# Two entries of a fused encoder layer reordered: norm, T2 and B11 ahead of weight sums and B22; token loads ahead of residual rows and later weight rows

## The chip, the core and the metric

The kernel runs on one NeuronCore of a Trainium2 chip. TensorE (PE) multiplies, VectorE (DVE), ScalarE (ACT) and GpSimd (POOL) do the elementwise work, and all loads and stores are issued in order by SyncE (SP), whose queue feeds 16 DMA engines. The metric is device time in microseconds (us) of one execution, the median over runs.

## The reference

One layer of a streaming encoder runs over 1024 prompt tokens and 8 x 16 sample tokens, 1152 token columns in all, model width 1024, in fp32. The change touches the second half of the layer:

```
x = x + g1 * mix                                   # residual after the output projection
h = rms_norm(x, norm_ffn) * (1 + sc2) + sh2        # per-token norm, modulation
up, ffn_new = causal_dwconv(h @ w_up, ffn_prev, conv_ffn_w, conv_ffn_b)
u, gt = jnp.split(up, 2, axis=-1)                  # 2816 columns each
x = x + g2 * ((jax.nn.silu(gt) * u) @ w_down)
```

## The kernel before, in words

Tokens lie along the free axis, features along the partitions. Every fp32 product is made of three passes over rounded operands: a value is split into a high part (cast on ACT) and a low part (value minus high part, on DVE), and PE adds high x high, low x high and high x low. A 128 x 576 product over 512 features is thus 24 matmuls (`product`).

Up projection. The 1024 x 1152 activations are cut into four quarters X11, X21 (first 576 tokens, features 0-511 and 512-1023) and X12, X22 (last 576 tokens). One Winograd-like step of seven products (P1 to P7) replaces eight. It needs the operands B11, B21, B22 (splits of X11, X21, X22) and T1 to T4 (splits of sums of quarters: T3 from X12 - after X22 - X12 -, T2 from X11 + that, T4 from X21 - T2, T1 from X22 - T2). `tsums` makes the sums, `halves` splits a quarter.

The first 768 tokens are complete before the last third (`out_proj(2, ...)`) is projected; their scaling, modulation and the splits of B11 and B21 are done piece by piece in `both`, which `hook` advances after each of that projection's eight outputs. The last third needs its own norm first (a column sum on PE, a power on POOL, a replication on PE, then `mod2` on DVE and ACT). Until T1 to T4 exist, PE is fed with the part of the work that needs B11 and B21 alone: `fill(0)` to `fill(5)`, each the P1 and P2 products of one early weight pair (48 matmuls). Then `Pair` objects run in the order `seq`; `prep` makes weight sums (`sums`) and splits (`wop`) up to LA = 3 steps ahead of `run`. The first products in `seq` are of pair 6: P1 (B11), P6 (T2), P5 (T1), P7 (T3), P2 (B21), P4 (T4).

P1, P6, P7 and P4 of a pair add to one PSUM bank, and each intermediate value is copied out by ACT (`evac` into a buffer of `tm4`) before the next product may add to it. The tile `tm4` takes one of the four quarter buffers when its quarter and T4's low part are no longer used; T1l, T3l and T4l take the other three.

Down projection. It is cut in the same way, over 11 pairs of feature blocks: `SEQ` runs P1, P6, P7, P4, P2, P5, P3, each for m = 0 to 10, 24 matmuls for each m. `dload` loads the gated activations `gd` (into the five `raw` buffers, two for each m of P6) and, for P1, P6 and P7, the rows of w_down: WA in P1 (names wa), WB[m][1] (wbh) and WB[m][0] (wbl). `dprep` makes sums and splits. After P1, P6 and P7 the four accumulators are copied to `pbuf`; `fma` later adds them to residual rows, which `resid` loads from DRAM (1152 KB each, xr). A residual load was traced at m = 6 and the `fma` steps at m = 1 to 4 of the next product.

The order on each engine isn't that of the code. A scheduler places the traced instructions by priorities and readiness; `tc.issue_after(ins)` obliges it to place what the block traces on the engine of `ins` behind `ins`. Each engine then runs its list strictly in its order.

Of the kernel before, what the change touches and what calls it, by code (L numbers as in the profile page):

```python
# [10 lines left out]
ALU = mybir.AluOpType  # L11
# [9 lines left out]
HT = 576  # L21
# [3 lines left out]
KD = 11  # L25
# [14 lines left out]
def body(ctx, tc, d):  # L40
    nc = tc.nc
    V, S, G_, T = nc.vector, nc.scalar, nc.gpsimd, nc.tensor
# [258 lines left out]
    def traced():  # L301
        return nc.cur_bb.bb.instructions[-1]
# [532 lines left out]
    h = [R(), R()]  # L835
# [80 lines left out]
    def quarter(nm, dt=F32):  # L916
        return ha.tile([P, 4, HT], dt, name=nm, tag="X", bufs=4)

    X11, X21, X12, X22 = (quarter("X" + n) for n in ("11", "21", "12", "22"))
    M2 = mod[:, 24:32, :]  # L920

    def split(op, x, ks):
        S.copy(op[0][:, ks, :], x[:, ks, :])  # L923
        V.tensor_tensor(op[1][:, ks, :], x[:, ks, :], op[0][:, ks, :].bitcast(F32), op=ALU.subtract)

    def tsums(c):
        V.tensor_tensor(X12[:, :, c], X22[:, :, c], X12[:, :, c], op=ALU.subtract)
        V.tensor_tensor(X11[:, :, c], X11[:, :, c], X12[:, :, c], op=ALU.add)
        V.tensor_tensor(X21[:, :, c], X21[:, :, c], X11[:, :, c], op=ALU.subtract)

    def both():
        for g in range(2):
            for kt in range(8) if g == 0 else scaled(1):
                xs = x1k[g][kt // 4][:, kt % 4, :]
                x1, x2 = ((X11, X12), (X21, X22))[kt // 4]
                parts = [(x1[:, kt % 4, 0:GN], xs)] if g == 0 else [
                    (x1[:, kt % 4, GN:HT], xs[:, 0:192]), (x2[:, kt % 4, 0:192], xs[:, 192:GN])]
                for o, x in parts:
                    S.activation(o, x, AF.Identity, bias=M2[:, kt, 0:1])
# [28 lines left out]
    fso = wt([P, 44, 18], "fso")  # L968

    nops = [0]  # L970
    cur, evs = [], {}

    def wop(x):
        i = nops[0] % 2
# [30 lines left out]
    def fill(j):  # L1005
        u = rawt()
        nc.sync.dma_start(out=u[:, :1024], in_=d["w_up"][2 * j])
        X = bank("P1")
        product(X, wop(u[:, 0:512]), B11)
        pc = wt([P, NT], "uy", 2)  # L1010
        p, c = pc[:, 0:HT], pc[:, HT:NT]
        S.copy(two(p), bk(X))
        nc.sync.dma_start(out=p1d[j], in_=p)
        Y = bank("P2")
        product(Y, wop(u[:, 512:1024]), B21)
        V.tensor_tensor(two(c), two(p), bk(Y), op=ALU.add)
        nc.sync.dma_start(out=c11d[j], in_=c)
# [17 lines left out]
    def halves(nm, x, l):  # L1035
        h = hi[nm]
        for k0 in (0, 2):
            split((h, l), x, slice(k0, k0 + 2))
        return h, l

    fill(0)
    fill(1)
    rb = bank("rst")
    for t in range(3):
        T.matmul(rb[:, 0, t:t + 1], ss2[:, t * P:(t + 1) * P], C["ones"][:, 0:1], start=True, stop=True)
    r2 = rstd2[:, 2, :]
# [9 lines left out]
    tsums(slice(192, HT))  # L1056
    fill(4)
    T2 = halves("T2", X11, hi["T2l"])
    B22 = halves("B22", X22, hi["B22l"])
    V.tensor_tensor(X22, X22, X11, op=ALU.subtract)  # L1060
    fill(5)
    T1 = halves("T1", X22, quarter("T1l", F32R))
    T3 = halves("T3", X12, quarter("T3l", F32R))
    T4 = halves("T4", X21, quarter("T4l", F32R))
    tm4 = quarter("tm4")
# [146 lines left out]
    for i in range(len(seq)):  # L1212
        while loaded < len(firsts) and firsts[max(loaded - 1, 0)] <= i + 1:
            seq[firsts[loaded]][0].load()
            loaded += 1
        while prepped < min(len(seq), i + 1 + LA):
            seq[prepped][0].prep(seq[prepped][1])
            prepped += 1
        seq[i][0].run(seq[i][1])
    hs_.close()  # L1220
# [19 lines left out]
    def wload(k, t, c):  # L1240
        nc.sync.dma_start(out=t, in_=d["w_down"][k, :, c])

    def dload(s):
        n, m = SEQ[s]
        if n == "P1":
            wload(K1[m], WA[m][:, lo_], lo_)
        raws[s] = []
        for kk, c in SRC[n]:
            r = rawt()
            nc.sync.dma_start(out=r[:, :HT], in_=gd[kk[m], :, c])  # L1250
            raws[s].append(r)
        if n == "P1":
            wload(K1[m], WA[m][:, hi_], hi_)
        elif n == "P6":
            wload(K2[m], WB[m][1], hi_)
        elif n == "P7":
            wload(K2[m], WB[m][0], lo_)

    def bop(x):
        h = dl.tile([P, HT], F32R, name="gh", tag="gh", bufs=4)  # L1260
# [44 lines left out]
    def advance(upto):  # L1305
        ev = None
        while st["prepped"] < min(len(SEQ), upto):
            while st["loaded"] < min(len(SEQ), st["prepped"] + 4):
                n, m = SEQ[st["loaded"]]
                if held() + len(SRC[n]) > 5:  # L1310
                    break
                dload(st["loaded"])
                st["loaded"] += 1
            ev = dprep(st["prepped"])
            st["prepped"] += 1
        return ev

    def resid(t, r, c):
        nc.sync.dma_start(out=t, in_=x1d[:, 4 * r:4 * r + 4, c])
        return t  # L1320
# [55 lines left out]
    for s in range(nt):  # L1376
        n, m = SEQ[s]
        advance(s + 1 + LA)
        if m == 0 and n in ("P1", "P2", "P5"):
            acc = [bank("acc") for _ in range(4)]  # L1380
        if m == 6 and n in ("P1", "P6", "P7"):
            xr[HOME[n]] = resid(xrs.pop(0), *HOME[n])
        if m == 6 and n == "P4":
            xr[FIN[n]] = resid(pbuf, *FIN[n])
        if 0 < m <= 4 and hold:
            h, p = hold[0]
            fma(xr[h][:, m - 1, :], m - 1, *h, p=p[:, m - 1, :])
            if m == 4:
                hold.clear()
        if s < nt - TAIL:  # L1390
            for o in range(4):
                dmul(acc, s, o)
        elif s == nt - 1:
            for o in range(4):
                for q in range(nt - TAIL, nt):
                    dmul(acc, q, o)
        if m < KD - 1:
            continue
        if n in HOME:
# [117 lines left out]
```

## Time and profile before

| | |
|---|---|
| median of 3 runs | 1293.63 us (1288.19 to 1293.78) |
| the profiled execution's own time | 1292.55 us |
| its span, first to last instruction | 1290.3 us |
| mean granted TensorE clock | 0.979 |
| PE busy / DVE / ACT / POOL | 96% / 75% / 49% / 15% of the span |
| DMA | 218.71 MB, 49.4% of 16 engines' span in the hardware queue |

All times of the trace are counted from the span's start. 525 us is where the first `fill` product starts, 1030.6 us where the down projection starts. 2.25 us of the execution lie outside the span.

### The profile page before, as it was taken

How to read it: one execution, taken by the hardware profiler on the slowest of the kernel's cores; microseconds unless marked ns; L12 is line 12 of the kernel's file. 1: busy time of each engine (PE TensorE's matmuls, PEld its weight loads, DVE VectorE, ACT ScalarE, POOL GpSimd, SP SyncE). 2: the span in 40 equal slices, each digit the busy share in tenths (PEclk: the TensorE clock that was granted, in tenths of full speed). 3: DMA queues.
4: the chain of work that ended last, by engine and by line, in shares of the span. 5: the costliest groups of instructions: out<-in, count | busy, mean ns of one | idle time of the engine just before them, and what ended most of it. 6: DMA issues, size and time to landing. Idle time of an engine off the chain costs nothing.

```text
span 1290.3 us, 22870 instructions
## 1 busy us (share of the span) xinstructions
PE 1238.4 (96%) x8813; PEld 1161.9 (90%) x8813; DVE 962.3 (75%) x1920; ACT 627.7 (49%) x1111; POOL 193.8 (15%) x242
## 2 busy tenths in 40 slices
PE   5899989999999999989999999999999998999998
PEld 3698769888887999988999999999999997999998
DVE  3497798565885675796999888876867578986664
ACT  3367736665566534564444444545444444443332
POOL 0031554343420330000111101000000000000000
PEclk8999989999999989989999999999999998999999
DMA  8785443887586488621333232221212498434341
GB/s 321 285 289 197 153 147 123 289 288 265 196 301 251 151 288 315 201 97 59 106 106 103 96 109 91 83 92 62 94 53 73 150 357 293 123 110 152 122 129 60
DMA packets 87708, 218.71 MB, mean 170 GB/s; under 512 B 14928, under 2 KB 27344, under 8 KB 87600
## 3 DMA queue, kind: packets, MB, share of 16 engines
q1 hardware_dynamic: 87600, 217.26, 49.4%
q8 instruction: 69, 1.13, 0.4%
q14 instruction: 39, 0.32, 0.1%
HBM read 175.81 MB, written 41.42 MB: 168 GB/s over the span
## 4 chain that ended last, share of the span: by engine, by line
PE 80%; DVE 9%; DMA 6%; ACT 2%; issue 2%; POOL 0%; SPq 0%; DVEq 0%; ACTq 0%
PE P L990 36%; PE acc L1354 16%; PE s_f L305 3%; PE s_f L307 3%; PE s_f L306 3%; PE out_proj L305 2%; PE out_proj L306 2%; PE out_proj L307 2%; PE attn_o L547 1%; PE ada L154 1%; DMA wbh<-in_w_down 1%; DMA xs<-in_xT 1%; PE attn_t L534 1%; DVE PT L667 1%; PE s_q L305 1%
## 5 line engine op out<-in xcount | busy, mean ns | idle before, releaser
L990 PE MATMUL P<-T,wh 128*128 128x288 f32 x704 | 206.7, 296 | 7.4 <-ACT T L923 3.9
L990 PE MATMUL P<-T,wl 128*128 128x288 f32 x704 | 207.9, 296 | 0.0
L1354 PE MATMUL acc<-gh,wl 128*128 128x288 f32 x616 | 182.5, 299 | 0.7 <-DVE wl L981 0.7
L1354 PE MATMUL acc<-gh,wh 128*128 128x288 f32 x616 | 176.6, 298 | 5.2 <-ACT wh L979 5.2
L1354 PE MATMUL acc<-gl,wh 128*128 128x288 f32 x616 | 179.6, 297 | 0.0
L990 PEld LDWEIGHTS P<-T,wh 128*128 128x128 f32 x704 | 132.5, 189 | 8.3 <-ACT tm L1133 4.2
L990 PEld LDWEIGHTS P<-T,wl 128*128 128x128 f32 x704 | 133.2, 189 | 0.0
L1097 DVE SCALAR_TENSOR_TENSOR uy<-uraw,fw,uy 128x1024 f32<-128x1024 f32 x88 | 112.2, 1278 | 22.9 <-ACT uy L1094 22.9
L981 DVE TENSOR_TENSOR wl<-raw,wh 128x512 fp32r<-128x512 f32 x143 | 94.9, 685 | 38.2 <-ACT wh L979 38.2
L1354 PEld LDWEIGHTS acc<-gh,wh 128*128 128x128 f32 x616 | 115.0, 190 | 5.6 <-ACT wh L979 5.6
L1354 PEld LDWEIGHTS acc<-gh,wl 128*128 128x128 f32 x616 | 117.5, 191 | 0.9 <-DVE wl L981 0.9
L1354 PEld LDWEIGHTS acc<-gl,wh 128*128 128x128 f32 x616 | 117.0, 191 | 0.0
L81 ACT CAST wh<-raw 128x1024 fp32r<-128x1024 f32 (+1 forms) x72 | 75.8, 1053 | 57.8 <-PE out_proj L307 30.7
L979 ACT CAST wh<-raw 128x512 fp32r<-128x512 f32 x143 | 83.4, 620 | 38.6 <-PE P L990 34.2
L1262 ACT CAST gh<-raw 128x576 fp32r<-128x576 f32 x66 | 44.4, 675 | 111.8 <-PE acc L1354 94.0
L1263 DVE TENSOR_TENSOR gl<-raw,gh 128x576 fp32r<-128x576 f32 x66 | 49.7, 756 | 50.0 <-ACT gh L1262 49.7
L1133 ACT COPY tm<-P 128x576 f32<-128x576 f32 x47 | 29.8, 635 | 113.7 <-PE P L990 102.6
L305 PE MATMUL s_f<-Rh,wh 128*128 128x384 f32 x240 | 83.2, 347 | 0.0
L307 PE MATMUL s_f<-Rl,wh 128*128 128x384 f32 x240 | 82.2, 342 | 0.0
L306 PE MATMUL s_f<-Rh,wl 128*128 128x384 f32 x240 | 81.8, 341 | 0.0
L1099 POOL COPY fso<-uraw 128x2 f32<-128x2 f32 x44 | 13.3, 303 | 447.7 <-DVE uraw L1082 447.7
L305 PE MATMUL out_proj<-Rh,wh 128*128 128x384 f32 x192 | 67.8, 354 | 0.9 <-ACT qn L424 0.9
(382 smaller groups left out, 3549.1 us busy)
## 6 DMA issues: line engine op xcount, KB each, us to landing
raw<-in_w_up SPq DMA_DIRECT2D x50, 512.0 KB, 3.4
raw<-gd SPq DMA_DIRECT2D x88, 288.0 KB, 2.8
raw<-in_w_ada SPq DMA_DIRECT2D x32, 512.0 KB, 5.8
raw<-in_w_f SPq DMA_DIRECT2D x30, 512.0 KB, 6.2
gd<-uy SPq DMA_DIRECT2D x22, 576.0 KB, 3.2
raw<-in_w_out SPq DMA_DIRECT2D x24, 512.0 KB, 5.1
wl<-low_f SPq DMA_DIRECT2D x20, 512.0 KB, 4.5
raw<-in_w_ad SPq DMA_DIRECT2D x16, 512.0 KB, 5.6
```

The costliest lines, as they stand in the source:

```text
L81: S.copy(wh[:, :n], raw[:, :n])
L305: T.matmul(ps, lh, rh, start=first, stop=False)
L306: T.matmul(ps, ll, rh, start=False, stop=False)
L307: T.matmul(ps, lh, rl, start=False, stop=last)
L979: S.copy(h, x)
L981: V.tensor_tensor(l, x, h.bitcast(F32), op=ALU.subtract)
L990: T.matmul(ps[:, c, 0:HC], x[:, m], y[:, kt, cc], start=first and kt + n == 0, stop=kt == 3 and n == 2, skip_group_check=True)
L1097: V.scalar_tensor_tensor(y[:, :1024], raw[:, j:j + 1024], k[:, j:j + 1], y[:, :1024], op0=ALU.mult, op1=ALU.add)
L1133: S.copy(two(dst), bk(ps))
L1262: S.copy(h, x)
L1263: V.tensor_tensor(l, x, h.bitcast(F32), op=ALU.subtract)
L1354: T.matmul(acc[o][:, c, 0:HC], x[:, oc], y[:, cc], start=first and i == 0, stop=m == KD - 1 and i == 2, skip_group_check=True)
```

## The change

At the first entry `both` goes through one feature block of both token groups at a time; the last term of `tsums` (X21, for T4) becomes `tsum4`; the norm's column sum is traced between `fill(0)` and `fill(1)`; X21, B22 and X22 are placed behind T2, weight steps 0 to 2 behind T2, and all later ones behind T1. At the second entry the rows wbh are loaded four m earlier in P1 (m > 3) and the remaining ones in P6, the residual rows are loaded at P6 m = 1, P7 m = 1, P7 m = 8 and P4 m = 7 instead of P1, P6, P7 and P4 m = 6, and the `fma` steps move from m = 1..4 to m = 7..10 (m = 3..6 in P4). The arithmetic is the same.

```diff
     def tsums(c):
         V.tensor_tensor(X12[:, :, c], X22[:, :, c], X12[:, :, c], op=ALU.subtract)
         V.tensor_tensor(X11[:, :, c], X11[:, :, c], X12[:, :, c], op=ALU.add)
+
+    def tsum4(c):
         V.tensor_tensor(X21[:, :, c], X21[:, :, c], X11[:, :, c], op=ALU.subtract)
 
     def both():
-        for g in range(2):
-            for kt in range(8) if g == 0 else scaled(1):
+        s1 = scaled(1)
+        for kt in range(8):
+            for g in range(2):
+                if g == 1:
+                    next(s1)
...
     fill(0)
-    fill(1)
     rb = bank("rst")
     for t in range(3):
         T.matmul(rb[:, 0, t:t + 1], ss2[:, t * P:(t + 1) * P], C["ones"][:, 0:1], start=True, stop=True)
     r2 = rstd2[:, 2, :]
     V.tensor_scalar(r2, rb[:, 0, 0:3], 1.0 / 1024, EPS, op0=ALU.mult, op1=ALU.add)
     G_.tensor_tensor(r2, r2, C["expo"][:, :3], op=ALU.pow)
+    fill(1)
...
     T2 = halves("T2", X11, hi["T2l"])
-    B22 = halves("B22", X22, hi["B22l"])
-    V.tensor_tensor(X22, X22, X11, op=ALU.subtract)
+    ev2 = traced()
+    with tc.issue_after(ev2), tc.issue_after(evs["ACT"]):
+        tsum4(slice(192, HT))
+        B22 = halves("B22", X22, hi["B22l"])
+        V.tensor_tensor(X22, X22, X11, op=ALU.subtract)
     fill(5)
     T1 = halves("T1", X22, quarter("T1l", F32R))
+    ev1 = traced()
...
         while prepped < min(len(seq), i + 1 + LA):
-            seq[prepped][0].prep(seq[prepped][1])
+            with tc.issue_after(ev2 if prepped < 3 else ev1):
+                seq[prepped][0].prep(seq[prepped][1])
...
+        evs["SP"] = traced()
         if n == "P1":
             wload(K1[m], WA[m][:, hi_], hi_)
-        elif n == "P6":
-            wload(K2[m], WB[m][1], hi_)
-        elif n == "P7":
-            wload(K2[m], WB[m][0], lo_)
+        with tc.issue_after(evs["SP"]):
+            if n == "P1" and m > 3:
+                wload(K2[m - 4], WB[m - 4][1], hi_)
+            elif n == "P6" and m < 4:
+                wload(K2[m + 7], WB[m + 7][1], hi_)
+            elif n == "P7":
+                wload(K2[m], WB[m][0], lo_)
...
-        if m == 6 and n in ("P1", "P6", "P7"):
-            xr[HOME[n]] = resid(xrs.pop(0), *HOME[n])
-        if m == 6 and n == "P4":
-            xr[FIN[n]] = resid(pbuf, *FIN[n])
-        if 0 < m <= 4 and hold:
+        for h in {("P6", 1): [HOME["P1"]], ("P7", 1): [HOME["P6"]], ("P7", 8): [HOME["P7"]]}.get((n, m), []):
+            with tc.issue_after(evs["SP"]):
+                xr[h] = resid(xrs.pop(0), *h)
+        m0 = 3 if n == "P4" else KD - 4
+        if m0 <= m < m0 + 4 and hold:
             h, p = hold[0]
-            fma(xr[h][:, m - 1, :], m - 1, *h, p=p[:, m - 1, :])
-            if m == 4:
+            with tc.issue_after(evs["DVE"]):
+                fma(xr[h][:, m - m0, :], m - m0, *h, p=p[:, m - m0, :])
+            if m == m0 + 3:
                 hold.clear()
```

Where the rows stand on the engines. VectorE around the last third's norm, before (uy is a `fill` result, rstd2 the norm's sum, wl a low part of weights, S1 a weight sum, L1023 the first step of `mod2`):

```order
L1016 TENSOR_TENSOR uy_5624<-uy_5624,P2_5627 128x576
L981 TENSOR_TENSOR wl_5817<-raw_5813,wh_5816 128x512 x2
L1016 TENSOR_TENSOR uy_5687<-uy_5687,P2_5690 128x576
L1047 TENSOR_SCALAR rstd2_91<-rst_5719 128x3
L981 TENSOR_TENSOR wl_5883<-raw_5879,wh_5882 128x512 x2
L1125 TENSOR_TENSOR S1_6136<-raw_6035 128x512
L1023 SCALAR_TENSOR_TENSOR X12_5197<-X12_5197,A2_80,rst_5719 128x256 x4
```

The same place after the change (L1032 is the first step of `mod2`):

```order
L1025 TENSOR_TENSOR uy_5624<-uy_5624,P2_5627 128x576
L1086 COPY uraw_6357<-cfc_6359 128x8x2
L1055 TENSOR_SCALAR rstd2_91<-rst_5656 128x3
L990 TENSOR_TENSOR wl_5817<-raw_5813,wh_5816 128x512 x2
L1025 TENSOR_TENSOR uy_5693<-uy_5693,P2_5696 128x576
L1032 SCALAR_TENSOR_TENSOR X12_5197<-X12_5197,A2_80,rst_5656 128x256 x4
```

The norm's sum stands ahead of the second `fill` result, and the sum S1 of a freshly loaded weight pair no longer stands ahead of `mod2`.

VectorE from T1 to T4, before (L1060 and L1072 are X22 - X11, the source of T1):

```order
L1060 TENSOR_TENSOR X22_5198<-X22_5198,X11_5195 128x2304
L924 TENSOR_TENSOR T2l_5592<-X11_5195,T2_5591 128x1152
L1016 TENSOR_TENSOR uy_5982<-uy_5982,P2_5985 128x576
L924 TENSOR_TENSOR T2l_5592<-X11_5195,T2_5591 128x1152
L981 TENSOR_TENSOR wl_6081<-raw_6030,wh_6080 128x512
L981 TENSOR_TENSOR wl_6081<-raw_6031,wh_6080 128x512
L924 TENSOR_TENSOR T1l_6014<-X22_5198,T1_5590 128x1152 x2
L1144 TENSOR_TENSOR raw_6030<-raw_6030 128x512
L924 TENSOR_TENSOR T3l_6019<-X12_5197,T3_5589 128x1152 x2
L1125 TENSOR_TENSOR S1_6328<-raw_6212 128x512
L924 TENSOR_TENSOR T4l_6024<-X21_5196,T4_5588 128x1152 x2
```

And after:

```order
L1025 TENSOR_TENSOR uy_5982<-uy_5982,P2_5985 128x576
L1072 TENSOR_TENSOR X22_5198<-X22_5198,X11_5195 128x2304
L1140 TENSOR_TENSOR raw_6030<-S1_6042,raw_6030 128x512
L927 TENSOR_TENSOR T1l_6014<-X22_5198,T1_5590 128x1152 x2
L990 TENSOR_TENSOR wl_6049<-raw_6031,wh_6048 128x512
L990 TENSOR_TENSOR wl_6081<-raw_6030,wh_6080 128x512
L990 TENSOR_TENSOR wl_6081<-raw_6031,wh_6080 128x512
L1138 TENSOR_TENSOR S1_6136<-raw_6035 128x512
L990 TENSOR_TENSOR wl_6039<-raw_6030,wh_6038 128x512
L927 TENSOR_TENSOR T3l_6019<-X12_5197,T3_5589 128x1152 x2
L1157 TENSOR_TENSOR raw_6030<-raw_6030 128x512
L1139 TENSOR_TENSOR raw_6035<-raw_6034,raw_6035 128x512
```

T2l and B22l stand further ahead now, and more weight rows stand between T1l and T4l, which follows one more weight row (S1_6328) after these. PE's own list keeps its products in the same order here, except that the second `fill` no longer starts inside the first and that only one B21 matmul instead of 24 stands between the second and the third matmul with T1.

At the down projection's entry, VectorE before (gl is a low part of tokens, L1328 the `fma` of P1's result, T2_0 to wl_11424 the first operands of P6):

```order
L1263 TENSOR_TENSOR gl_11428<-raw_11314,gh_11427 128x576
L1328 SCALAR_TENSOR_TENSOR xr_0_11068<-pbuf_11071,mod_75,xr_0_11068 128x576 x4
L1278 TENSOR_TENSOR T2_0_11072<-raw_11350,raw_11348 128x576
L1279 TENSOR_TENSOR raw_11350<-wbh_0_11050,wa_0_11039 128x512
L1263 TENSOR_TENSOR gl_11461<-T2_0_11072,gh_11460 128x576
L981 TENSOR_TENSOR wl_11424<-raw_11350,wh_11423 128x512
```

And after:

```order
L1281 TENSOR_TENSOR gl_11434<-raw_11320,gh_11433 128x576
L1296 TENSOR_TENSOR T2_0_11072<-raw_11357,raw_11355 128x576
L1297 TENSOR_TENSOR raw_11357<-wbh_0_11050,wa_0_11039 128x512
L1281 TENSOR_TENSOR gl_11467<-T2_0_11072,gh_11466 128x576
L990 TENSOR_TENSOR wl_11430<-raw_11357,wh_11429 128x512
L1296 TENSOR_TENSOR T2_1_11153<-raw_11426,raw_11424 128x576
```

P6's first operands follow P1's last ones directly; the `fma` steps stand some 40 rows further down, among P6's last and P7's first operands.

SP at the first P6 loads, before (raw_11348 and raw_11350 are those of m = 0, raw_11418 the first of m = 1):

```order
L1250 DMA raw_11348<-gd_67 128x576
L1241 DMA wbl_0_11061<-in_w_down 128x512
L1319 DMA xr_1_11069<-x1d_66 128x4x576
L1241 DMA wbl_1_11062<-in_w_down 128x512
L1241 DMA wbl_2_11063<-in_w_down 128x512
L1241 DMA wbl_3_11064<-in_w_down 128x512
L1241 DMA wbl_4_11065<-in_w_down 128x512
L1250 DMA raw_11350<-gd_67 128x576
L1241 DMA wbl_5_11066<-in_w_down 128x512
L1241 DMA wbl_6_11067<-in_w_down 128x512
L1319 DMA xr_2_11070<-x1d_66 128x4x576
L1250 DMA raw_11418<-gd_67 128x576
```

And after (raw_11355 and raw_11357 are the loads of m = 0, raw_11424 and raw_11426 those of m = 1):

```order
L1264 DMA raw_11355<-gd_67 128x576
L1264 DMA raw_11357<-gd_67 128x576
L1255 DMA wbh_7_11057<-in_w_down 128x512
L1122 DMA gd_67<-uy_11137 128x1152
L1264 DMA raw_11424<-gd_67 128x576
L1264 DMA raw_11426<-gd_67 128x576
L1255 DMA wbh_8_11058<-in_w_down 128x512
```

No residual row and no wbl row stands in SP's list now until the loads of P6 m = 5.

## Rows read from the trace of the kernel before

**Rows 1.** Stretches: us, busy time (count) of each engine, granted clock, DMA share, GB/s.

```profile
570.00:575.00 5.00, 1.09 (x3) 0.74 (x3) 5.00 (x5) 4.41 (x4) 0.00 (x0) 0.87 0.00 0
1070.00:1075.00 5.00, 5.00 (x21) 5.00 (x22) 1.02 (x2) 0.00 (x0) 0.00 (x0) 0.50 1.04 404
...
592.00:1030.00 438.00, 437.07 (x3308) 436.83 (x3309) 354.00 (x660) 204.71 (x309) 41.63 (x86) 1.00 0.28 92
1040.00:1078.00 38.00, 32.37 (x223) 31.68 (x221) 26.72 (x40) 10.98 (x19) 0.00 (x0) 0.91 1.05 389
```

**Rows 2.** Timeline of PE, first entry: start, us, instruction [idle before <- releaser].

```profile
525.20 0.29 PE L990 MATMUL P<-B11h,wh 128*128 128x288 f32 x1
...
528.35 0.29 PE L990 MATMUL P<-B21h,wh 128*128 128x288 f32 x1
...
584.16 0.29 PE L990 MATMUL P<-T1l,wh 128*128 128x288 f32 x1
586.50 0.40 PE L990 MATMUL P<-T,wh 128*128 128x288 f32 x1 [2.05 <-ACT tm L1133]
...
592.21 0.40 PE L990 MATMUL P<-T,wh 128*128 128x288 f32 x1 [0.73 <-ACT tm L1133]
```

**Rows 3.** Timeline of ACT and of POOL, first entry.

```profile
585.81 0.64 ACT L1133 COPY tm<-P 128x576 f32<-128x576 f32 x1 [11.09 <-DVE T4l L924]
...
541.06 1.23 POOL L1048 TENSOR_TENSOR rstd<-rstd,cst 128x3 f32<-128x3 f32 x1 [42.20 <-DVE rstd L1047]
```

**Rows 4.** Timeline of DVE, first entry.

```profile
547.03 0.69 DVE L1125 TENSOR_TENSOR S<-raw 128x512 f32<-128x512 f32 x1 [4.85 <-DMA raw<-in_w_up]
547.64 1.65 DVE L1023 SCALAR_TENSOR_TENSOR X<-X,A,rst 128x256 f32<-128x256 f32 x4
...
579.95 2.62 DVE L924 TENSOR_TENSOR T3l<-X,T 128x1152 fp32r<-128x1152 f32 x2
582.48 0.68 DVE L1125 TENSOR_TENSOR S<-raw 128x512 f32<-128x512 f32 x1
583.09 2.62 DVE L924 TENSOR_TENSOR T4l<-X,T 128x1152 fp32r<-128x1152 f32 x2
```

**Rows 5.** Chain that ended last, first entry: start, us, work.

```profile
544.54 0.67 PE rst L1050 x6
...
570.01 2.47 DVE X L1060
...
586.50 4.99 PE P L990 x24
```

**Rows 6.** Timeline of PE, down projection's entry.

```profile
1065.34 0.29 PE L1354 MATMUL acc<-gl,wh 128*128 128x288 f32 x1
1069.87 1.33 PE L1354 MATMUL acc<-gh,wh 128*128 128x288 f32 x4 [4.24 <-ACT wh L979]
...
1075.52 0.29 PE L1354 MATMUL acc<-gl,wh 128*128 128x288 f32 x1
...
1085.65 0.69 PE L1354 MATMUL acc<-gh,wh 128*128 128x288 f32 x4
```

**Rows 7.** Timeline of DVE, down projection's entry.

```profile
1056.24 1.42 DVE L1263 TENSOR_TENSOR gl<-raw,gh 128x576 fp32r<-128x576 f32 x2
1064.77 3.00 DVE L1328 SCALAR_TENSOR_TENSOR xr<-pbuf,mod,xr 128x576 f32<-128x576 f32 x4 [7.11 <-ACT pbuf L1402]
1067.69 0.75 DVE L1278 TENSOR_TENSOR T<-raw 128x576 f32<-128x576 f32 x1
...
1074.57 0.76 DVE L1278 TENSOR_TENSOR T<-raw 128x576 f32<-128x576 f32 x1 [3.98 <-DMA raw<-gd]
```

**Rows 8.** Timeline of SP's DMA issues, down projection's entry.

```profile
1065.92 5.02 SPq L1250 DMA_DIRECT2D raw<-gd  x4
```

**Rows 9.** DMA issues from 1010 to 1120 us: count, KB each, median us to landing.

```profile
xr<-x1d SPq DMA_DIRECT2D x3, 1152.0 KB, 8.4
...
wbl<-in_w_down SPq DMA_DIRECT2D x11, 256.0 KB, 8.3
```

More of the change, by code (lines that the diff above doesn't have):

```diff
@@ L920, in body @@
     M2 = mod[:, 24:32, :]
+    evs = {}
     def split(op, x, ks):
         S.copy(op[0][:, ks, :], x[:, ks, :])
+        evs["ACT"] = traced()
         V.tensor_tensor(op[1][:, ks, :], x[:, ks, :], op[0][:, ks, :].bitcast(F32), op=ALU.subtract)
@@ L943, in both @@
         tsums(slice(0, 192))
+        tsum4(slice(0, 192))
     todo = both()
@@ L970, in body @@
     nops = [0]
-    cur, evs = [], {}
+    cur = []
     def wop(x):
@@ L1313, in advance @@
                 st["loaded"] += 1
-            ev = dprep(st["prepped"])
+            ev = evs["DVE"] = dprep(st["prepped"])
             st["prepped"] += 1
@@ L1380, in body @@
             acc = [bank("acc") for _ in range(4)]
-        if m == 6 and n in ("P1", "P6", "P7"):
-            xr[HOME[n]] = resid(xrs.pop(0), *HOME[n])
-        if m == 6 and n == "P4":
-            xr[FIN[n]] = resid(pbuf, *FIN[n])
-        if 0 < m <= 4 and hold:
+        for h in {("P6", 1): [HOME["P1"]], ("P7", 1): [HOME["P6"]], ("P7", 8): [HOME["P7"]]}.get((n, m), []):
[3 more added lines that the diff above has]
+        if m0 <= m < m0 + 4 and hold:
             h, p = hold[0]
-            fma(xr[h][:, m - 1, :], m - 1, *h, p=p[:, m - 1, :])
-            if m == 4:
+            with tc.issue_after(evs["DVE"]):
+                fma(xr[h][:, m - m0, :], m - m0, *h, p=p[:, m - m0, :])
+            if m == m0 + 3:
                 hold.clear()
+        if (n, m) == ("P4", 7):
+            with tc.issue_after(evs["SP"]):
+                xr[FIN[n]] = resid(pbuf, *FIN[n])
         if s < nt - TAIL:
```

## The prediction

> **What bounds the kernel now.** I read the granted clock and PE's busy share by stretches first, then PE's own timeline where that share drops, then the engine that PE waits for there, and last SP and the DMA queue.
>
> Between the two entries PE is busy for 437.07 of 438 us at full clock, with DVE at 354 us [rows 1]. There is nothing to win there but fewer matmuls, and the change takes none away. The time lies at the entries.
>
> First entry. A product is 24 matmuls, 0.131 us each: from 525.20 to 528.35 us is 3.15 us for one [rows 2]. From the first fill to the pair's first T3 matmul at 592.21 us [rows 2] PE's list has 380 matmuls, 49.8 us, and two short groups for the norm of about 0.6 us each (0.67 is shown [rows 5]). That is 51 us of work in 67 us: 16 us are lost. In 570 to 575 us PE has three matmuls in the records while DVE is busy for all 5 us [rows 1], so DVE is late. What releases PE at 586.50 us is ACT's copy of the first P1 result into tm [rows 2]; that copy waited 11.09 us for T4's low part on DVE [rows 3], because tm lives in the buffer that T4's source leaves. So the end of this entry is DVE's list up to T4l, which ends at 583.09 + 2.54 = 585.6 us [rows 4].
>
> Second entry. P1 of the down projection ends at 1065.47 us, P6 starts at 1069.87 after 4.24 us of idleness, its first product is at half clock and ends at 1075.65, and the fourth starts at 1085.65 [rows 6]. Three products at the full pace would have ended at 1065.47 + 9.43 = 1074.9: 10.7 us are lost. DVE shows why: it is done with P1's operands at 1057.66, then stands for 7.11 us at the `fma` of P1's result, which can't start before P1 has ended, and P6's first operand is queued behind it [rows 7]. The second operand waits 3.98 us more, for a load [rows 7]; SP issues it only at 1065.92 [rows 8], in a stretch of 38 us in which the DMA engines are full at 389 GB/s [rows 1].
>
> **The change part by part.**
>
> *Second entry, DVE.* The `fma` leaves its place. DVE's rows up to 1057.66 are the same set as before, without idleness among them, so P6's T2_0 can start there. The four steps of a product's operands take 0.67 + 0.61 + 0.67 + 0.61 = 2.6 us (start to start: 582.48 to 583.09 for a 512-wide row [rows 4]; two 576-wide ones take 1.42 us and one 0.75, so 0.67 for each further one [rows 7]). The first is ready near 1060.3, 5 us ahead of P1's end; each further one costs DVE 2.6 us against 3.15 us on PE.
>
> *Second entry, SP.* Three residual rows of 1152 KB and eleven wbl of 256 KB [rows 9] leave the full stretch: 6.4 MB, at 389 GB/s 16.5 us of transfers that P6 didn't need. The load of P6 m = 0 then stands behind P1's last loads alone and goes out when a raw buffer is free, by DVE's rows near 1050 us; m = 1 near 1055.5. P6 itself needs 2 x 288 + 256 KB for each m, 2.2 us at 389 GB/s, less than PE's 3.15. I take the whole loss but for 0.2 us (ACT's copies of P1's accumulators stand between P6's casts now): **10.5 us**. Bounds: 10.7 above; below, 5 us, if P6's operands come as they are needed rather than ahead.
>
> *Where the residual rows go.* A row lands after 8.4 us at full DMA load [rows 9]; by SP's list the first is issued when P6 is near m = 3 (an estimate), and the `fma` needs it four or more products (12.6 us) later. The `fma` steps cost DVE the same time as before. I cost this at nothing; the cover is DVE's lead of about three products, 9.4 us. Without it each late row would stop DVE's list, and PE with it.
>
> *First entry, norm.* The norm's sum now follows 48 matmuls instead of 96, and the replicated norm comes after 48 more: 525.20 + 6.3 + 0.35 (wait for B21's last piece, an estimate: DVE's list has it near 530) + 0.6 + 6.3 + 0.67 = 539.4, against 545.2 [rows 5]. The power on POOL, 1.23 us [rows 3], hides behind the 48 matmuls. DVE no longer stands 4.85 us for a weight load just ahead of `mod2` [rows 4]. `mod2` starts near 539.5 instead of 547.64 [rows 4]: 8.1 us earlier.
>
> *First entry, DVE's list from `mod2` to T4l.* It took 585.63 - 547.64 = 38.0 us [rows 4]. Its new form has five more weight rows in this stretch (two low parts, two S1 sums, one further sum) and two fewer: 3 x 0.61 = 1.8 us more, 39.8 us. Two waits are new. X22 - X11 stands behind the last fill's result; PE ends that product eight products after the norm, 539.4 + 25.2 + 0.2 = 564.8, and DVE, with 15.5 us of the 39.8 still ahead of it (2.47 [rows 5], three pairs of splits of 2.53 and nine rows of 0.61 [rows 4]) and 0.67 for the result itself, would be there at 563.1: 1.6 us. And T1l waits for ACT's cast of X22 (2.47 us on DVE [rows 5]), where T2l stood between before: 0.5 us. T4l ends at 539.5 + 39.8 + 2.1 = 581.4, against 585.6; T2 on PE starts 0.8 us later, at 582.2 against 586.50: 4.3 us earlier. T2 and B22 change places at no price, since neither is what PE waits for.
>
> *What is late next.* PE has finished T1 and the B21 product by about 576.5 and stands 5.7 us instead of 2.05 us [rows 2]. Then the clock counts. After 4.24 us of idleness a whole product ran at half clock, 5.8 us [rows 6], at 0.50 granted [rows 1]; the T2 product after 2.05 us took 4.99 us [rows 5]. I add 0.8 us: **3.5 us** remain. The Trainium skill, "TensorE: Matmul & The Clock Gate", "HAM oscillation — how this bites in real kernels", says that gaps on PE bring the slow clock back; by that rule, too, a longer gap speaks against this part, and the trace agrees (0.50 after the gap). Bounds: 6.3 us above (8.1 less 1.8, no wait new); 0 below, if S1_6328's weights, whose buffer is free only behind T1l now, hold T4l up by another 3.5 us.
>
> **Sum.** 10.5 + 3.5 = 14.0 us. The profiled execution took 1292.55 us, so 1278.5. It stands 1.1 us under the median of three, which also has a run at 1288.19; I keep 1278.5.
>
> **Rivals.**
>
> 1. *The first entry gives nothing* (0 bound): T4l still ends near 585, by the load or by weight rows moved ahead of it. For it: DVE's work there grows. Against: its start is 8 us earlier by PE's own list. 1282.
> 2. *The first entry gives all*: no new wait and no cold product, 6.3 us, and the second 10.7. Against: PE must stand for T4l anyhow. 1275.5.
> 3. *The put-off transfers come back.* Residual rows and wbl now run beside P6's and P7's loads; 8.4 us to landing against a lead of 9.4 us is near. One stall of 5 us with its cold product (2.7 us) leaves 14 - 7.7 = 6.3: 1286. For it: five raw buffers hold two and a half m of P6. Against: the 16.5 us of transfers spread over the 100 us from P6 to P4, and P6 needs the engines for 2.2 of 3.15 us. The Trainium skill, "DMA: Bandwidth & Descriptors", "Issuing engines are not separate DMA queues", says that all transfers share the same 16 engines; by that rule a new order adds no bandwidth and only puts bytes off; the trace agrees so far as that the engines were full at 389 GB/s with all kinds of loads among them.
> 4. *Slower*: DVE stops at the moved `fma` in P6, P7 and P4 for a residual row, with the next operands behind it. It decides from 14 + 6.5 = 20.5 us on, 6.8 us at each of three places; nothing in the rows shows such a wait where the load is issued 12 us ahead. 1299 and more.
> 5. *Not what it says*: both entries keep their losses because something else ends last, a buffer of wh or gh in P6, T4l in the first. 1290 to 1293.
>
> **How the numbers follow.** The sum 0.56, rival 1 0.13, rival 2 0.12, rival 3 0.10, rival 5 0.06, rival 4 0.03. Half a per cent, 6.5 us, is about what can be told from no change here. The sum and rivals 1 and 2 are faster by more, rival 3 nearly always: 0.90; same 0.07; slower 0.03. The range goes from 1273 (rival 2 with 2 us of scatter between runs) to 1285 (rival 1 with 3 us).
>
> **What would show it.** Right: `mod2` on DVE near 539.5, T4l's end near 581.4, PE's T2 near 582 after a gap of over 5 us and at half clock; T3's first matmul 6.5 us after T2's (5.7 before), near 588.7; at the second entry no gap at all between P1 and P6, the clock at 1.00, DVE without a wait for pbuf, P6's fourth product 9.4 us after P1's end. Wrong: a gap on PE after P6 has begun, with DVE standing at L1346 or a load of gd; T4l later than 583; a wait in P1 for wa, now that wbh rows stand among them.

## The result and the profile after

The changed kernel takes 1276.6 us (median of 4 runs, 1272.99 to 1278.2) against 1292.68 us of the kernel before (4 runs, one more than in the section on its time): a ratio of 0.9878, 95% interval 0.9845 to 0.9912. In a later group of runs it took 1277.06 us (6 runs), with a ratio of 0.9879 (0.9853 to 0.9904). The forecast was 1278.5 us. The profiled execution took 1277.79 us, 14.76 us less than the profiled one of before.

PE's landmarks split these 14.76 us. First rows of the kernel after, then the two of before that [rows 2] doesn't have: the first `fill`, the first pair's T2 and T3, the down projection's first matmul and its last.

```profile
524.34 0.29 PE L999 MATMUL P<-B11h,wh 128*128 128x288 f32 x1
...
582.04 0.61 PE L999 MATMUL P<-T,wh 128*128 128x288 f32 x1 [5.25 <-ACT tm L1146]
...
588.05 0.40 PE L999 MATMUL P<-T,wh 128*128 128x288 f32 x1 [0.73 <-ACT tm L1146]
...
1026.47 0.56 PE L1372 MATMUL acc<-gh,wh 128*128 128x288 f32 x3
...
1270.77 0.29 PE L1372 MATMUL acc<-gl,wh 128*128 128x288 f32 x1
```

```profile
1030.60 0.56 PE L1354 MATMUL acc<-gh,wh 128*128 128x288 f32 x3
...
1285.52 0.29 PE L1354 MATMUL acc<-gl,wh 128*128 128x288 f32 x1
```

From the first fill to T3: 588.05 - 524.34 = 63.71 us, before 67.01 [rows 2], so 3.3 us. From the down projection's first matmul to its last: 244.30 us, before 254.92, so 10.6 us. 0.86 us lie ahead of the first fill (524.34 against 525.20); the experiments show that this is scatter between executions.

Stretches of the kernel after, as in [rows 1]:

```profile
570.00:575.00 5.00, 4.68 (x33) 4.44 (x34) 5.00 (x8) 0.26 (x1) 0.00 (x0) 1.00 0.18 34
...
580.00:585.00 5.00, 2.96 (x12) 2.96 (x13) 3.71 (x5) 0.64 (x1) 0.00 (x0) 0.50 0.19 62
...
1025.00:1050.00 25.00, 25.00 (x192) 25.00 (x191) 24.96 (x40) 16.31 (x26) 0.78 (x2) 1.00 0.99 341
...
1060.00:1065.00 5.00, 5.00 (x40) 5.00 (x39) 4.27 (x7) 4.04 (x8) 0.00 (x0) 1.00 0.63 176
1065.00:1070.00 5.00, 5.00 (x40) 5.00 (x40) 4.90 (x9) 2.90 (x5) 0.00 (x0) 1.00 0.93 298
```

At the second entry PE is busy for all 5 us of every stretch and the clock stays at 1.00; in the first the clock falls to 0.50, 1.2 GHz, behind T2's wait of 5.25 us. All that PE waits for from 500 us on (engine, line and what it waited for: sum, times, longest) now lies at the first entry, but for 0.2 us ahead of it and 0.73 at the end of the up projection (one of the three for `tm`); no wait of `acc` is left:

```profile
PE P L999 <- ACT tm L1146: 6.7, 3, 5.3
PE P L999 <- ACT T L925: 1.4, 1, 1.4
PE P L999 <- DVE T1l L927: 0.9, 2, 0.7
PE out_proj L306 <- DMA wl<-low_o: 0.2, 1, 0.2
```

DVE's timeline at the first entry, as in [rows 4]:

```profile
539.00 1.65 DVE L1032 SCALAR_TENSOR_TENSOR X<-X,A,rst 128x256 f32<-128x256 f32 x4
...
554.46 2.63 DVE L927 TENSOR_TENSOR T2l<-X,T 128x1152 fp32r<-128x1152 f32 x2 [1.45 <-ACT T L925]
...
568.72 2.63 DVE L927 TENSOR_TENSOR T1l<-X,T 128x1152 fp32r<-128x1152 f32 x2 [0.61 <-ACT T L925]
...
578.62 2.62 DVE L927 TENSOR_TENSOR T4l<-X,T 128x1152 fp32r<-128x1152 f32 x2
581.16 0.68 DVE L1140 TENSOR_TENSOR raw<-S,raw 128x512 f32<-128x512 f32 x1
```

ACT's, as in [rows 3]. Its list has T3's cast (the row at 550.64) ahead of T2's (553.28); DVE's T2l waits for the second:

```profile
550.64 2.21 ACT L925 CAST T<-X 128x1152 fp32r<-128x1152 f32 x2 [1.57 <-DVE X L930]
552.76 0.61 ACT L988 CAST wh<-raw 128x512 fp32r<-128x512 f32 x1
553.28 2.21 ACT L925 CAST T<-X 128x1152 fp32r<-128x1152 f32 x2
...
581.35 0.64 ACT L1146 COPY tm<-P 128x576 f32<-128x576 f32 x1 [11.09 <-DVE T4l L927]
```

DVE's timeline at the second entry, as in [rows 7]: P6's first row, its longest wait for a load, and the first `fma`.

```profile
1053.45 0.75 DVE L1296 TENSOR_TENSOR T<-raw 128x576 f32<-128x576 f32 x1
...
1074.34 0.76 DVE L1296 TENSOR_TENSOR T<-raw 128x576 f32<-128x576 f32 x1 [3.15 <-DMA raw<-gd]
...
1089.23 0.81 DVE L1346 SCALAR_TENSOR_TENSOR xr<-pbuf,mod,xr 128x576 f32<-128x576 f32 x1
```

SP's issues, as in [rows 8]: the loads of P6's first operand, and the first residual row, now behind them.

```profile
1048.61 3.40 SPq L1264 DMA_DIRECT2D raw<-gd  x2
...
1064.49 0.38 SPq L1337 DMA_DIRECT2D xr<-x1d  x1
```

### The profile page after: what moved, and what is told of

Same layout as the page of the kernel before. It is cut to its first block, busy times and chain, and to the rows that moved or that the text cites. A ratio compares the mean times of both kernels' runs of the same rounds, so it can differ in the third digit from the quotient of the medians.

```text
span 1275.6 us, 22879 instructions
## 1 busy us (share of the span) xinstructions
PE 1232.2 (97%) x8813; PEld 1155.2 (91%) x8813; DVE 963.1 (76%) x1920; ACT 627.4 (49%) x1111; POOL 195.0 (15%) x242
## 4 chain that ended last, share of the span: by engine, by line
PE 84%; DVE 8%; DMA 3%; ACT 2%; issue 1%; POOL 0%; SPq 0%; DVEq 0%; ACTq 0%
PE P L999 37%; PE acc L1372 19%; PE s_f L305 3%; PE s_f L307 3%; PE s_f L306 3%; PE out_proj L305 2%; PE out_proj L306 2%; PE out_proj L307 2%; PE attn_o L547 1%; PE ada L154 1%; PE attn_t L534 1%; DVE PT L667 1%; PE s_q L305 1%; PE s_q L306 1%; PE s_q L307 1%
```

## The experiments

All kernels' landmarks, read as above (us; "again" is the same kernel in a later group). Fill to T3 and fill to down cover the first entry, down to last the second. A ratio is to runs of the kernel before in the same group (medians of 1291.15 to 1292.68 us). The rows are those of one profiled execution each.

| kernel | median (lowest to highest), runs | ratio to before, 95% | first fill | fill to T3 | fill to down | down to last |
|---|---|---|---|---|---|---|
| before | 1292.68 (1288.19 to 1293.78), 4 | | 525.20 | 67.01 | 505.40 | 254.92 |
| after | 1276.6 (1272.99 to 1278.2), 4 | 0.9845 to 0.9912 | 524.34 | 63.71 | 502.13 | 244.30 |
| after, again | 1277.06 (1272.6 to 1282.32), 6 | 0.9853 to 0.9904 | 519.37 | 63.51 | 501.92 | 244.68 |
| e1_first | 1288.38 (1285.16 to 1290.17), 10 | 0.9955 to 0.9987 | 523.44 | 63.77 | 502.19 | 255.26 |
| e2_second | 1280.62 (1277.89 to 1281.58), 4 | 0.9899 to 0.9948 | 521.52 | 66.63 | 505.05 | 244.28 |
| e3_fma | 1288.96 (1285.97 to 1292.23), 10 | 0.9968 to 0.9997 | 522.47 | 63.78 | 502.20 | 255.36 |
| e4_w | 1284.05 (1282.31 to 1286.16), 6 | 0.9920 to 0.9963 | 524.87 | 63.92 | 502.34 | 251.20 |
| e3b | 1282.58 (1279.26 to 1284.79), 4 | 0.9896 to 0.9943 | 524.83 | 63.53 | 501.94 | 250.99 |
| e6_norm | 1279.98 (1277.55 to 1281.33), 4 | 0.9891 to 0.9949 | 521.32 | 66.49 | 504.91 | 244.31 |
| e7_order | 1276.51 (1276.11 to 1278.97), 4 | 0.9869 to 0.9919 | 523.38 | 62.97 | 501.39 | 244.31 |
| e5_p | 1273.83 (1270.63 to 1277.53), 4 | 0.9839 to 0.9901 | 521.67 | 58.00 | 496.40 | 245.49 |
| e5_p, again | 1274.66 (1274.11 to 1276.46), 5 | 0.9845 to 0.9886 | 522.79 | 58.00 | 497.92 | 246.88 |
| e5_pu | 1275.18 (1274.18 to 1278.41), 4 | 0.9857 to 0.9911 | 525.14 | 57.96 | 496.12 | 246.01 |
| e8_both | 1270.16 (1268.65 to 1273.3), 5 | 0.9809 to 0.9849 | 523.92 | 60.7 | 496.87 | 245.49 |

### Each entry alone

*e1_first* has the program up to `lp_.close()` from after and the rest from before; *e2_second* the other way round.

> Only the first entry as changed; the down projection (weights, residual rows, fma) as before. Theory: the two entries don't touch, so this one keeps what the changed kernel gained up to the start of the down projection (its first matmul at 1026.47 against 1030.60 us: 4.1 us, of which 0.9 us stood already at the first fill, 524.34 against 525.20) and loses the 10.6 us of the second (last matmul at 1270.77 against 1285.52, 14.75 in all): P1 to P6 with a gap of over 4 us on PE and a product at half clock, time 1288 to 1289.5 us. If the 0.9 us at the first fill is scatter of the profiled execution and no work of the change, the first fill comes near 525.2 here or in the next kernel. Rival: part of the second entry's gain came from the first (a down projection that starts earlier finds its loads later, or sooner): then this kernel stands more than 2 us away from that.

> Only the second entry as changed; everything up to the down projection as before. Theory: 10.6 us less than before, 1282 us; T2 of the first pair on PE near 586.5 and T3 near 592.2 as before, no gap on PE between P1 and P6, clock 1.00 there. Rival (the gains are not separate): over 1285 or under 1279.

Both came as the theory said, if e2's places are counted from its first fill: 1288.38 and 1280.62 us. The sums of the stages add up: e1 has the first entry of after (63.77) and the second of before (255.26), e2 the reverse (66.63 and 244.28). So these two gains don't touch each other. The first fill stands at 521.52 in e2, whose code up to there is that of before: the 0.86 us are scatter. By the times the first entry brings 0.13 to 0.45%, 1.7 to 5.8 us, by the rows 2.9 (66.63 less 63.71) to 3.3.

### The second entry taken apart

*e3_fma* keeps the `fma` in its later place and puts the loads back, all but the fourth residual row (the one into `pbuf`); *e3b* puts only the weight rows back:

```
-        with tc.issue_after(evs["SP"]):
-            if n == "P1" and m > 3:
-                wload(K2[m - 4], WB[m - 4][1], hi_)
-            elif n == "P6" and m < 4:
-                wload(K2[m + 7], WB[m + 7][1], hi_)
+        elif n == "P6":
+            wload(K2[m], WB[m][1], hi_)
...
-        for h in {("P6", 1): [HOME["P1"]], ("P7", 1): [HOME["P6"]], ("P7", 8): [HOME["P7"]]}.get((n, m), []):
+        if m == 6 and n in ("P1", "P6", "P7"):      (e3_fma only)
```

*e4_w* keeps the weight rows' new order and puts back the `fma` (`0 < m <= 4`) with the residual rows it needs.

> The changed kernel, but loads in the down projection (weight rows, residual rows) in the order of before; the fma stays in its later place. Theory (two blocks that stand side by side, so that either alone keeps most of the loss): DVE doesn't stand for pbuf, P6's first operand is there by P1's end, but the load of the second is issued only near 1061.8 us and lands near 1070, PE goes on with P6 m=1 near 1074 against 1064.5 without loss: 9 to 10.5 us of the 10.6 lost, time 1286 to 1287. Rival (the fma's wait is the cause and the loads only came late because their buffers were held): 1277 to 1279.

> The changed kernel, but fma and residual rows in the down projection where they were before; only the weight rows (wbh, wbl) keep their new order. Theory: P6's loads are there, DVE stands for pbuf until P1's end as before, P6's first matmul comes 4.2 to 4.5 us after P1's end, its first product runs at half clock (2.65 us more), the second follows without a wait: 7 us of the 10.6 lost, time 1283.5. Rival (loads are the cause, the fma's wait is hidden behind operands that are ready ahead): 1277 to 1279. Rival (three residual rows still fill the queue): as late as before, 1287.

> The changed kernel, but the weight rows of the down projection (wbh, wbl) in the order of before; fma and residual rows in their new places. Theory (what made P6's operands late beside the fma is bytes ahead of them, 3.4 MB of residual rows, 8.9 us at 389 GB/s, and 4.6 us of wbl): with the residual rows gone the second operand's load lands 6 to 9 us sooner than with only the fma moved; 0 to 4 us of the 11 are lost, 1277 to 1281. Rival (the weight rows do it): as with only the fma moved, 1287 and more.

e3_fma: 1288.96 us, all of the 11 us lost again (255.36 against 244.30), a little more than the 9 to 10.5 expected. DVE no longer stands for `pbuf`, and stands for the loads in its place. The expectation had P6's first operand there by P1's end; it was late too, by a load that DVE waited 9.00 us for. Its timeline, P6's first and second operand, and PE's:

```profile
1061.32 0.76 DVE L1293 TENSOR_TENSOR T<-raw 128x576 f32<-128x576 f32 x1 [9.00 <-DMA raw<-gd]
...
1068.58 0.76 DVE L1293 TENSOR_TENSOR T<-raw 128x576 f32<-128x576 f32 x1 [4.35 <-DMA raw<-gd]
```

```profile
1063.51 1.33 PE L1369 MATMUL acc<-gh,wh 128*128 128x288 f32 x4 [3.80 <-ACT wh L988]
...
1070.77 0.80 PE L1369 MATMUL acc<-gh,wh 128*128 128x288 f32 x4 [1.28 <-ACT wh L988]
```

e4_w: 1284.05 us. The loads are there, DVE stands for `pbuf`, and PE waits once; its rows and DVE's:

```profile
1066.48 1.33 PE L1372 MATMUL acc<-gh,wh 128*128 128x288 f32 x4 [4.25 <-ACT wh L988]
```

```profile
1061.37 3.01 DVE L1346 SCALAR_TENSOR_TENSOR xr<-pbuf,mod,xr 128x576 f32<-128x576 f32 x4 [5.83 <-ACT pbuf L1420]
```

251.20 - 244.30 = 6.9 us: the 4.25 us, and 2.65 for a product at half clock. So the later `fma` without the new order of the loads gains nothing, the weight rows alone (with the `fma` as before) 4 us (251.20 against 255.26 in e1_first), both together 11: two waits that lie side by side, of which the one left keeps its whole length.

e3b missed: 1282.58 us where 1277 to 1281 were expected, and 6.7 us of the second entry lost where 0 to 4 were. PE's rows show what the expectation left out, and DVE's the second:

```profile
1063.65 0.98 PE L1369 MATMUL acc<-gh,wh 128*128 128x288 f32 x4 [1.82 <-ACT wh L988]
...
1098.53 0.40 PE L1369 MATMUL acc<-gh,wl 128*128 128x288 f32 x1 [0.69 <-DVE wl L990]
...
1173.04 0.37 PE L1369 MATMUL acc<-gh,wh 128*128 128x288 f32 x1 [1.59 <-DVE pbuf L1341]
```

```profile
1172.08 2.99 DVE L1341 SCALAR_TENSOR_TENSOR pbuf<-acc,mod,pbuf 128x576 f32<-128x576 f32 x4 [1.83 <-DMA pbuf<-x1d]
```

A gap of only 1.82 us still brought the lower clock (0.75 in 1065 to 1070 us), and the fourth residual row, which goes into `pbuf` at the end of P4, landed 1.83 us late. Counted matmul by matmul against the changed kernel, 2.0 us are lost at the first gap, 1.8 in the product behind it, 1.1 in the rest of P6 and in P7, most of it at the wait of 0.69, and 1.8 at the end of P4. So the lower clock cost less here than the 2.5 us that the product behind e4_w's gap lost, by the same count.

### The first entry taken apart

*e6_norm* puts the norm's sum behind `fill(1)` again, all else as changed. *e7_order* keeps the norm early and puts back the places of T2, B22 and the weights. Both keep the new order inside `both`:

```
-    ev2 = traced()
-    with tc.issue_after(ev2), tc.issue_after(evs["ACT"]):
-        tsum4(slice(192, HT))
-        B22 = halves("B22", X22, hi["B22l"])
-        V.tensor_tensor(X22, X22, X11, op=ALU.subtract)
+    B22 = halves("B22", X22, hi["B22l"])
+    V.tensor_tensor(X22, X22, X11, op=ALU.subtract)      (free to go ahead of T2; tsum4 again ahead of fill(4))
...
-            with tc.issue_after(ev2 if prepped < 3 else ev1):
-                seq[prepped][0].prep(seq[prepped][1])
+            seq[prepped][0].prep(seq[prepped][1])
```

> The changed kernel, but the norm's sum stands behind the second fill again (T2, B11, the weights' order and the whole second entry as changed). Theory (the first entry's gain is the earlier start of DVE's list, mod2): mod2 some 5.7 us later behind the first fill, DVE has 1.9 us of rows done ahead of it, T4l's end 2.5 to 4 us later: first fill to first T3 66.2 to 67.8 us against 63.7 to 63.9 (before 66.6 to 67.0), time 1279 to 1281. Rival (the order of T2, B22 and the weights is what gained): within 1 us of 63.8.

> The changed kernel with the norm early, but B22 ahead of T2 and the pairs' weights free to go ahead, as before. Theory (the norm's place is what counts): mod2 14.7 us behind the first fill as in the changed kernel, DVE's rows from there to T4l's end 40.3 us by the rows' durations (39.7 in the changed kernel), first fill to first T3 62.5 to 64.5 us, time within 1.5 us of the changed kernel's. Rival (without the new order weight loads and casts stand in DVE's way again): 66 us and more, 1279 and more.

e6_norm: 1279.98 us and 66.49 us from fill to T3, almost what before has (66.63 and 67.01). e7_order: 1276.51 us, as the changed kernel, and 62.97 us. The times alone would not tell e6_norm from the changed kernel, since the intervals overlap; the rows do, as the changed first entry has 63.51 to 63.92 in six executions. The gain of the first entry needs the norm's place, and the new order of T2, B22 and the weights brings nothing. Whether the norm's place would bring as much without the new order in `both` was not run. DVE's rows of e7_order show why it is even 0.7 us ahead by the rows:

```profile
538.03 1.65 DVE L1032 SCALAR_TENSOR_TENSOR X<-X,A,rst 128x256 f32<-128x256 f32 x4
...
576.17 2.62 DVE L927 TENSOR_TENSOR T4l<-X,T 128x1152 fp32r<-128x1152 f32 x2
```

38.14 us from `mod2` to T4l, without a wait between; 39.62 us in the changed kernel (578.62 - 539.00), where T2l and T1l wait for ACT for 1.45 and 0.61 us.

### What holds T2: the buffer

*e5_p* copies the first pair's P1 result into a `uy` buffer, so that it needs no buffer that T4's source leaves (`uy` are two buffers that also hold the `fill` results); *e5_pu* does the same with the result after T2. *e8_both* is e5_p on top of e7_order.

```
-                q.p = tmp()
+                q.p = wt([P, NT], "uy", 2)[:, :HT] if q.j == order[0] else tmp()
...
-                q.U2 = wt([P, NT], "uy", 2)[:, :HT] if q.j == NF - 1 else tmp()
+                q.U2 = wt([P, NT], "uy", 2)[:, :HT] if q.j in (NF - 1, order[0]) else tmp()      (e5_pu only)
```

> The changed kernel, but the first pair's P1 result is copied into a uy buffer instead of tm4, whose buffer T4's source leaves. Theory (T4l's end on DVE holds T2 through that buffer alone): PE goes on with T2 when T1 and the B21 product are done, 5.25 us earlier than 582.04; its result still goes into tm4 and waits for T4l's end near 581.2, so T3 starts near 582.1 against 588.05, perhaps with a product at a lower clock behind a gap of 2 us: 4 to 6 us less, 1271 to 1273 us. Rival (T2 waits for its own operands or weights, or DVE's list just gets later by as much): T2 within 1 us of 582, no gain, 1276 to 1277.

> As the kernel with P1's result in uy, and the result after T2 goes into a uy buffer too. Theory: T3 follows T2 without a wait for T4l, near 580.7 against 588.05, at full clock; 7.4 us less than the changed kernel, 1269 to 1270. Rival: the two uy buffers are missing for the first pair's convolutions, and PE stands there later: no better than the kernel with one, over 1272.

> The kernel with P1's result in a uy buffer once more, beside the changed kernel. Its profile gave 5.7 us at the first entry and lost 1.2 in the down projection, 4.5 in all, where the medians of two different calls lay 2.8 apart. If the 4.5 us are real: a median 3.5 to 5.5 us under the changed kernel's of this group. Rival (what is won at the entry is lost again): within 1.5 us.

> Norm early, P1's result in a uy buffer, but B22 ahead of T2 and the weights free, as in the kernel with the old order. Theory (the new order of T2, B22 and weights brings nothing; T4l's end sets T3): T4l ends near 56 us behind the first fill, T3 near 57 against 58.0 with the new order and 63.7 in the changed kernel; 5.5 to 7 us under the changed kernel. Rival (with the gap gone the new order counts, since T1 and T2 are then waited for): T3 later than 58.0.

> The changed kernel once more, beside the others of this group on one chip. 1276 to 1278; first fill to first T3 matmul 63.7 to 63.9 us, down projection 244.3 us.

e5_p: T3 stands 58.00 us behind the first fill, 5.7 us sooner than in the changed kernel, with no wait for `tm` ahead of T2 and 0.57 us ahead of T3. PE's rows of e5_p:

```profile
566.45 0.40 PE L999 MATMUL P<-T,wh 128*128 128x288 f32 x1 [1.82 <-ACT T L925]
...
579.67 0.40 PE L999 MATMUL P<-T,wh 128*128 128x288 f32 x1 [0.57 <-ACT tm L1146]
...
1158.84 0.37 PE L1372 MATMUL acc<-gh,wh 128*128 128x288 f32 x1 [0.59 <-ACT gh L1280]
```

So the buffer was the cause. But the down projection loses 1.2 us (245.49), in the second group 2.6 (246.88). PE's rows have one new wait in each, of 0.59 and of 0.69 us. The rest stands in the rows of PE's weight loads (PEld), which show shorter waits: 0.27 and 0.80 us in e5_p, and 0.35, 0.93, 0.26, 0.38 and 0.35 in its second execution, 1.07 and 2.27 us together. Most are for DVE. The one of 0.80 us belongs to P2's first product: in e5_p, e5_pu and e3b that starts 0.96 to 0.97 us behind DVE's first step on `pbuf`, whichever engine PE's row names, and in all three DVE had waited for the residual row in `pbuf`. PEld's rows of e5_p with DVE's, then the longest one of the second execution:

```profile
1089.17 0.19 PEld L1372 LDWEIGHTS acc<-gl,wh 128*128 128x128 f32 x1 [0.27 <-DVE gl L1281]
...
1157.87 2.99 DVE L1344 SCALAR_TENSOR_TENSOR pbuf<-acc,mod,pbuf 128x576 f32<-128x576 f32 x4 [0.83 <-DMA pbuf<-x1d]
...
1158.81 0.19 PEld L1372 LDWEIGHTS acc<-gh,wh 128*128 128x128 f32 x1 [0.80 <-issue]
```

```profile
1089.23 0.19 PEld L1372 LDWEIGHTS acc<-gh,wl 128*128 128x128 f32 x1 [0.93 <-DVE wl L990]
```

In the second group the stretch behind T3 was 1.5 us longer as well (497.92 - 58.00 against 496.40 - 58.00): there T3 came behind 2.14 us of waiting, at a granted clock of 0.66. The first group's median, 1273.83, was to be 1271 to 1273. In the times of the second group 2.4 us are left, between 1274.66 and 1277.06 us, with intervals that overlap. What was expected for the group, 3.5 to 5.5 us, did not come, the rival's 1.5 neither: about half of what is won at the entry is given back.

e5_pu missed: 1275.18 us where 1269 to 1270 were expected. T3 stands 57.96 us behind the first fill, no sooner than in e5_p. PE's list has 11 matmuls with B21 between T2 and T3 (1.4 us), so T3 could not follow at once; and T1 ran at a granted clock of 0.53 (570 to 575 us) behind a wait of 1.82 us. DVE waited 1.36 us for the residual row in `pbuf`, as in e3b.

e8_both has the lowest median, 1270.16 us; its interval (0.9809 to 0.9849) lies below that of the changed kernel in the same group (0.9853 to 0.9904), by a hair. Its stages are 4.2 us shorter (496.87 + 245.49 against 501.92 + 244.68), its median 6.9; the rest stands in no stage that the change touches (the two profiled executions took 1273.3 and 1273.0 us, with first fills at 523.92 and 519.37), and may be scatter. Not all came as expected. T4l ends 56.0 us behind the first fill, as forecast, but T3 stands at 60.7, past the 58.0 that the rival named: PE takes T2 before T1 now, begins a second product with T2 ahead of T3, and stands there 2.59 us for weight rows that DVE has behind T4l, the next thing to move. e5_p, with the new order, has no such wait. Yet from fill to down projection e8_both's length (496.87) lies between those of e5_p's two executions (496.40 and 497.92), so here too the new order shows no gain. PE's row and DVE's:

```profile
580.65 0.40 PE L999 MATMUL P<-T,wl 128*128 128x288 f32 x1 [2.59 <-DVE wl L990]
```

```profile
577.38 2.62 DVE L927 TENSOR_TENSOR T4l<-X,T 128x1152 fp32r<-128x1152 f32 x2
579.91 1.28 DVE L990 TENSOR_TENSOR wl<-raw,wh 128x512 fp32r<-128x512 f32 x2
```

## Why the prediction was right

*Second entry, DVE and SP* (10.5 us forecast, 10.6 measured). The forecast put P6's first row at 1057.66, 27.06 us behind the down projection's first matmul; it stands at 1053.45, 26.98 behind. PE has no gap and the clock stays up. Theory and bounds were right, and e3_fma and e4_w show what the prediction only implied: it counted one loss with two causes and did not share it out between them. Any fixed shares would have been wrong, since 0 and 4 us, each alone, make 11 together.

*Residual rows at nothing.* Right for PE, which waits for none. The three rows in `xr` come in time: the first is issued at 1064.49, lands 8.3 us later and is needed at 1089.23, 16.4 us after that. But the cover was sized wrong, and what it had to cover was not the row itself. The prediction had a lead of DVE over PE of 9.4 us. The low part of the weights of P6 m = 5 is ready some 6 us ahead of PE, and that of m = 6 only 1.8 us (1078.72, needed near 1080.55), because the operand loads behind the first residual row take a median of 7.4 us to land where those ahead of it take 2.9. In e4_w, whose residual rows stand elsewhere, the median stays between 2.9 and 3.2 us through P6. DVE's row of the changed kernel, and its loads issued from 1058 to 1064 and from 1066 to 1070 us:

```profile
1078.03 0.69 DVE L990 TENSOR_TENSOR wl<-raw,wh 128x512 fp32r<-128x512 f32 x1
```

```profile
raw<-gd SPq DMA_DIRECT2D x3, 288.0 KB, 2.9
```

```profile
raw<-gd SPq DMA_DIRECT2D x4, 288.0 KB, 7.4
```

The fourth row, into `pbuf`, is as thin: issued at 1156.96 us, landed 5.6 us later, needed at 1165.01, so 2.4 us to spare. In e7_order the same row took 7.6 us to land, and some 0.6 us were left. It came late in e3b (1.83 us of waiting), e5_pu (1.36) and e5_p (0.83). The mechanism of rival 3 exists, then, and costs 1 to 3 us where it shows, not 7.7.

*First entry* (3.5 us forecast, 2.9 to 3.3 measured). Counted from the first fill: `mod2` forecast at 14.3 us, measured 14.66. T4l's end, 41.9 us later by forecast, came 42.16 later (581.16 - 539.00). Of the two new waits the first was elsewhere: the forecast had 1.6 us ahead of X22 - X11 for the last fill's result, and DVE waited 1.45 us at T2l instead, because ACT casts T3's half first, and so came to the result no earlier than PE. The second, T1l's, was forecast at 0.5 and measured 0.61. The product of T2 took 5.3 us from its start to the copy of its result (587.36 - 582.04), not 5.8: the clock cost 0.3 us more than before, not 0.8. So T2 stood 0.7 us later behind the first fill than forecast (57.70 against 57.0) and its product took 0.5 us less: that the part came within 0.6 us is in part luck, as two misses nearly cancel. The Trainium skill's rule ("TensorE: Matmul & The Clock Gate", "HAM oscillation — how this bites in real kernels") that gaps bring the slow clock back held: 0.50 behind 5.25 us. Shorter waits did so too, in some executions (last section).

*What the prediction left open* was how much of the first part belongs to which edit. It charged 1.8 us of additional rows and 2.1 us of waits to the new order of T2, B22 and weights; e7_order has about the same rows without that order (38.14 us against 39.62 less 2.06 of waits), so the rows are no price of that order; the waits, which are gone there, are one, and it has no return.

*Rivals.* 1 (first entry gives nothing) falls by e1_first, 2 (all) by the 5.25 us that PE still stands, 4 (slower) by the first moved `fma`, which DVE starts without a wait (1089.23), 5 by both entries.

## What to carry to other kernels

Where two things make the same operand late, an `fma` queued ahead of it and loads ahead of its own, undoing one may give nothing (0 and 4 us here) and both 11: list all that ends near the same time before an edit is priced. Where PE waits for a copy, ask whose buffer the copy goes into: one tile elsewhere was worth 5.7 us at its place, more than moving the norm. And a transfer that is put off has to be followed to its new place: read there the time to spare of the row itself (2.4 us at `pbuf`) and of the loads behind it (1.8 us in P6). All four executions with P1's result in `uy` lost 1.2 to 2.6 us in the down projection, much of it at these two places; no run shows why their loads came later.

## What the runs showed of the hardware that was not expected

The same short waits bring the lower clock in one execution and not in another. A granted clock between 0.50 (1.2 GHz) and 1.00 (2.4 GHz) is the mean over its stretch. In the changed kernel waits of 1.45, 0.73 and 0.18 us around 570 us left it at 1.00 in 570 to 575 us (row above). e5_p waits 1.82 and 0.73 us there; in its first profile the clock was then at 0.73, and PE ran 31 matmuls in 5 us in which it runs 40 at full clock. In its second profile, with the same two waits, it stayed at 1.00, and fell only behind 2.14 us, ahead of T3. The first profile's row, and two of the second:

```profile
570.00:575.00 5.00, 5.00 (x31) 5.00 (x30) 5.00 (x7) 0.00 (x0) 0.00 (x0) 0.73 0.36 108
```

```profile
570.00:575.00 5.00, 4.95 (x38) 4.78 (x37) 5.00 (x8) 0.00 (x0) 0.00 (x0) 1.00 0.33 105
...
580.00:585.00 5.00, 4.21 (x20) 4.21 (x21) 3.74 (x7) 1.22 (x2) 0.00 (x0) 0.66 0.56 164
```

And the start of the first fill scatters from 519.37 to 525.20 us between the profiled executions (519.37 to 524.87 among the six with the changed first entry), more than the first entry's gain, while the length of the stage behind it repeats to 0.4 us in those six (63.51 to 63.92). With few runs, a stage is compared by its own length and not by the end of the span.
